# Scan of a hybrid decoder kernel on one Trainium2 core: step sizes loaded two chunks ahead, the sample sum ahead of the state decay on GpSimd, the first output tile's upper products first, the last convolution put off

## The chip, the cores and the metric

The kernel runs on one core of one Trainium2 chip. A core has five engines that each work through an instruction queue of their own, in order: TensorE (PE in the profile; its weight loads are PEld), VectorE (DVE), ScalarE (ACT), GpSimd (POOL) and SyncE (SP). They wait for one another by semaphores. SP and POOL issue the transfers between the chip's memory (HBM) and on-chip memory (SBUF), which 16 DMA engines carry out. Products come out in PSUM. The metric is the device time of one execution in microseconds (us); the median of the runs is compared.

## The reference: what is computed

One inference step of a small decoder trunk: a Mamba-2 (SSD) layer and a pooling layer, for 1024 new tokens of one sequence (the prompt) and 8 new tokens of each of 8 sequences (the samples), together 1088 token columns. The width is 1024, the inner width 2048, in 32 heads of 64 in 8 groups of 4, with a state of 128. All data are float32. The part of the reference that this case is about, cut:

```python
zxbcdt = h @ w_in                                # z, x, B, C, dt
conv = conv_b + sum(xp[:, k:k + L] * conv_w[k] for k in range(4)); xbc = silu(conv)
# scan, chunks of T = 128 tokens, for each group g of 4 heads
acum = cumsum(dt * A)                            # within a chunk
y_intra = einsum('bctgn,bcsgn->bctsg', C, B) * decay  @ xdt
chunk_states = einsum(B, exp(acum[-1] - acum), xdt)
h_c+1 = exp(acum[-1]) * h_c + chunk_states       # from chunk to chunk
y = y_intra + einsum(C, exp(acum), h_prev) + d_skip * x
gated = rmsnorm over the 256 columns of a group of (y * silu(z))
x = x + (1 + gate) * (gated @ w_out)
```

The samples' 64 columns are the ninth chunk (chunk 8): they start from given states h0 (8 sequences), which are decayed, added to and given back as new states.

## The kernel before, in words

Products in float32 are made of three products of rounded halves: upper times upper, lower times upper, upper times lower (`mm3`, lines 182 to 184; matmul weights wh and wl are the halves of a weight tile, gh and gl or hh and hl those of the activations). A product of 128 output rows has three column pieces of 368, 368 and 352 (CH), each in a PSUM tile `mm`, of which there are three.

The SSD layer runs group after group, 0 to 7 (`scan_group`). Beside the scan of groups 0 to 4, PE makes the input projection of later groups, each of four tiles (x, x, B, C) with a convolution on DVE and ACT behind it (`conv_tile`, lines 356 to 362; `proj_evict` moves the product out of PSUM on ACT, L419 and L421, and then calls `proj_end`, which makes the convolution). Beside the scan of groups 5 to 7, PE makes the output projection of the groups that are done, in parts of four k tiles (`op_units`, `op_unit`): for an output tile d and a column piece 12 matmuls, then the eviction into x on DVE (L771 to L776). The k tiles come back from HBM (gr), are split into gh on ACT (L749) and gl on DVE (L750), and the x tiles of the residual are loaded two output tiles ahead (L1528).

A group's scan takes its nine chunks two by two. For a chunk, `front` reads the step sizes (acb, a broadcast load of 256 KB, L533 and L536), makes exp of them on ACT (ea, L548), transposes on PE (tr, L554 and L557), masks the decay (M), scales x (xd) on DVE, and copies Bt out on ACT (L574); `states` sums the chunk states S (L596) and carries them on (hd on GpSimd, L604, then h on DVE, L605); `rows` makes the output rows y (L617, L621). For chunk 8 the columns are first copied into xp tiles on GpSimd (L436). `sample_inter` multiplies the given states with C (Z, L636) and scales (zsc on DVE, L639). `back_sample` adds xdt to zsc on GpSimd (L645), from which PE makes the samples' rows (L650), and decays the given states h0 on GpSimd, 128 x 1024 twice (L653). `state_sample` adds the samples' contributions to them (L670 on PE, L673 on DVE) and stores them (hsT, L675). The group's norm follows: y times z (L709), squares (L710), their sum (L711), its row sums ms on PE (L715), the rows' scale rs, which goes through HBM and comes back (L720, L723), and the scaled rows (L727).

Tiles of SBUF come from pools: a tile's buffer is given to the next tile of its tag when all readers of the old one are through, and a load into it waits for that. Large tiles (x, xbc, z, h0, gr, gh, gl) share slots, so that which tile comes after which depends on the order in which they are asked for and freed.

The order of instructions on each engine is set by a scheduler of the framework, which takes the instructions as the generators of scan and products issue them, turn by turn, weighs them with estimates of its own, and fixes one order for each engine; at run time an engine only waits. `issue_after(ins)` lays what is issued under it behind the instruction `ins`.

## Time and profile before

| | us |
|---|---|
| median of 3 runs | 1618.24 (1616.37 to 1619.92) |
| the profiled execution | 1620.23 |
| its span, first to last instruction | 1618.5 |
| PE busy | 1581.7 (98%) |
| DVE busy | 1288.2 (80%) |
| ACT busy | 796.5 (49%) |
| POOL busy | 500.8 (31%) |

The scan runs from about 330 to 950 us of the span. In the profile's timelines a row has the start in us, the duration, the engine, the line of the kernel, the operation, the tile written and those read, the sizes and the count; in brackets the idle time of the engine just before, and what ended it. Waits are rows of an engine and line, what was waited for, the sum in us, how often, and the longest. The granted clock is 1.00 at full speed.

### The profile page before, as it was taken

The numbers are of one execution on the slowest core, as the hardware profiler recorded it, in microseconds if no ns is written. First come the engines' busy times: TensorE is split into PE (matmuls) and PEld (weight loads), VectorE is DVE, ScalarE is ACT, GpSimd is POOL, SyncE is SP. The second block draws the span as 40 slices with busy tenths as digits, with TensorE's granted clock in tenths as the row PEclk, the third lists the DMA queues.
The fourth block names the chain that finished last, engine by engine and source line by source line (L and its number), as shares of the span: only waits on it lengthen the run. The fifth ranks groups of instructions, "written<-read, shape, count | busy, mean of one in ns | idle before, by whom it ended". The sixth has DMA issues, their size and how long they took to land. (4 is left out here: it accounts for less than half of the span.)

```text
span 1618.5 us, 30648 instructions
## 1 busy us (share of the span) xinstructions
PE 1581.7 (98%) x11916; PEld 1506.4 (93%) x11916; DVE 1288.2 (80%) x2148; ACT 796.5 (49%) x1517; POOL 500.8 (31%) x562
## 2 busy tenths in 40 slices
PE   8999999999999999999999999999999999999997
PEld 6799999998889889888898899999999999999997
DVE  5875779778888888788888867988889867577886
ACT  6653344357676766674555436623223233333364
POOL 0133556421221212120212222365666640000241
PEclk8999999999999999999999999999999999999999
DMA  9422232354555454668898632133333379555683
GB/s 344 169 85 91 94 117 69 110 186 139 201 161 175 157 192 148 234 210 300 293 338 279 216 128 93 45 139 115 106 106 103 115 223 364 164 165 180 160 176 120
DMA packets 122305, 275.58 MB, mean 170 GB/s; under 512 B 18192, under 2 KB 59312, under 8 KB 122160
## 3 DMA queue, kind: packets, MB, share of 16 engines
q1 hardware_dynamic: 118128, 260.90, 46.6%
q0 software_dynamic: 4032, 12.72, 4.5%
q8 instruction: 94, 1.54, 0.4%
q14 instruction: 51, 0.42, 0.1%
HBM read 201.12 MB, written 70.23 MB: 168 GB/s over the span
## 5 line engine op out<-in xcount | busy, mean ns | idle before, releaser
L989 PE MATMUL st<-hh,w 128*128 128x272 f32 x832 | 240.7, 289 | 2.1 <-DVE w L176 2.1
L987 PE MATMUL st<-hh,w 128*128 128x272 f32 x832 | 240.1, 289 | 0.0
L988 PE MATMUL st<-hl,w 128*128 128x272 f32 x832 | 239.9, 288 | 0.0
L987 PE MATMUL st<-t,w 128*128 128x272 f32 x624 | 179.7, 288 | 0.0
L989 PE MATMUL st<-t,w 128*128 128x272 f32 x624 | 179.5, 288 | 0.0
L182 PE MATMUL mm<-hh,wh 128*128 128x368 f32 (+1 forms) x528 | 178.7, 338 | 0.7 <-ACT raw L421 0.7
L988 PE MATMUL st<-t,w 128*128 128x272 f32 x624 | 179.2, 287 | 0.0
L183 PE MATMUL mm<-hl,wh 128*128 128x368 f32 (+1 forms) x528 | 173.6, 329 | 0.0
L184 PE MATMUL mm<-hh,wl 128*128 128x368 f32 (+1 forms) x528 | 173.4, 328 | 0.0
L989 PEld LDWEIGHTS st<-hh,w 128*128 128x128 f32 x832 | 156.4, 188 | 3.2 <-DVE w L176 3.2
L174 ACT ACTIVATE w<-wr 128x512 fp32r<-128x512 f32 x104 | 65.7, 631 | 188.8 <-PE st L989 155.5
L988 PEld LDWEIGHTS st<-hl,w 128*128 128x128 f32 x832 | 156.7, 188 | 0.0
L987 PEld LDWEIGHTS st<-hh,w 128*128 128x128 f32 x832 | 156.7, 188 | 0.0
L183 PE MATMUL mm<-gl,wh 128*128 128x368 f32 (+1 forms) x384 | 127.3, 331 | 3.6 <-DVE gl L750 3.5
L182 PE MATMUL mm<-gh,wh 128*128 128x368 f32 (+1 forms) x384 | 130.1, 340 | 0.6 <-ACT raw L419 0.5
L1204 PE MATMUL op<-b,w 128*128 128x272 f32 x448 | 128.9, 288 | 0.7 <-DVE b L1133 0.7
L1203 PE MATMUL op<-b,w 128*128 128x272 f32 x448 | 129.5, 289 | 0.0
L1205 PE MATMUL op<-b,w 128*128 128x272 f32 x448 | 128.9, 288 | 0.0
L184 PE MATMUL mm<-gh,wl 128*128 128x368 f32 (+1 forms) x384 | 127.0, 331 | 0.0
L604 POOL TENSOR_TENSOR hd<-h,cd 128x256 f32<-128x256 f32 x56 | 46.8, 836 | 233.2 <-DVE h L605 118.3
L987 PEld LDWEIGHTS st<-t,w 128*128 128x128 f32 x624 | 117.7, 189 | 0.1
L989 PEld LDWEIGHTS st<-t,w 128*128 128x128 f32 x624 | 117.3, 188 | 0.0
(298 smaller groups left out, 4544.6 us busy)
## 6 DMA issues: line engine op xcount, KB each, us to landing
wr<-win SPq DMA_DIRECT2D x48, 512.0 KB, 4.3
acb<-acd SPq DMA_DIRECT2D x64, 256.0 KB, 4.0
wr<-pin SPq DMA_DIRECT2D x32, 512.0 KB, 3.6
wr<-pout SPq DMA_DIRECT2D x28, 512.0 KB, 3.7
x<-x1d SPq DMA_DIRECT2D x24, 544.0 KB, 6.1
x1d<-x SPq DMA_DIRECT2D x22, 544.0 KB, 3.9
wr<-pout POOLq DMA_DIRECT2D x20, 512.0 KB, 5.7
x<-xT SPq DMA_DIRECT2D x16, 544.0 KB, 6.9
```

The costliest lines, as they stand in the source:

```text
L174: self.nc.scalar.activation(hi, src, AF.Copy)
L182: nc.tensor.matmul(ps[:, :n], hi[:, k, :], ah[:, a:a + n], start=first, stop=False)
L183: nc.tensor.matmul(ps[:, :n], hi[:, k, :], al[:, a:a + n], start=False, stop=False)
L184: nc.tensor.matmul(ps[:, :n], lo[:, k, :], ah[:, a:a + n], start=False, stop=last)
L604: nc.gpsimd.tensor_tensor(out=hd, in0=h[-1], in1=cd.unsqueeze(2).to_broadcast([P, 4, 64]), op=ALU.mult)
L987: nc.tensor.matmul(ps[c][:, :QUART], hi[:, k], xh[:, t], start=(k == 0), stop=False)
L988: nc.tensor.matmul(ps[c][:, :QUART], hi[:, k], xl[:, t], start=False, stop=False)
L989: nc.tensor.matmul(ps[c][:, :QUART], lo[:, k], xh[:, t], start=False, stop=(k == 3))
L1203: nc.tensor.matmul(ps[:, :QUART], hi[:, k], xh, start=k == 0, stop=False)
L1204: nc.tensor.matmul(ps[:, :QUART], hi[:, k], xl, start=False, stop=False)
L1205: nc.tensor.matmul(ps[:, :QUART], lo[:, k], xh, start=False, stop=k == 7)
```

## The change

It has five parts. (1) The step sizes acb get three buffers instead of two; two chunks are loaded at a group's start, and chunk c + 2 when chunk c is worked on. (2) The exponential ea is left out for chunk 0, where nothing reads it, and is made for chunk 8 on the 32 columns that are read; the three copies for chunk 8 go into the rest of that ea tile, so that they need the ring of ea and no tiles of their own. (3) In `back_sample` the add to zsc is issued first, and the two decays of h0 are laid behind it. (4) The first output tile (part 0, d = 0) is made by a new function, `op_first`: its three pieces at once, for each k tile the two products with the upper half of the activations, and only then the products with the lower halves. (5) The convolution of the last projected tile (group 6, the fourth) is not made behind its projection, but after output unit 7 of part 0 (the second piece of d = 2).

```diff
--- before.py
+++ after.py
@@ -24,6 +24,7 @@
 WINDOWS = tuple(2 << g for g in GROUPS)
 PARTS = ((0, 4), (4, 8), (8, 12), (12, 16))
 PREP = ((6, 10, 14, 18, 21), (9, 12, 15, 18, 21))
+LATE = 7
 XA = 2
 PLAIN = 2
 POOLW = (3, 5)
@@ -401,8 +402,9 @@
                     if k < 7:
                         yield
                 for c in range(3):
-                    self.proj_evict(G, ii, raw, ps[c], c)
+                    self.proj_evict(G, ii, raw, ps[c], c, False)
                 yield
+                self.late = lambda: self.proj_end(G, ii, raw, True)
                 return
             ada = self.ada_do(self.ada_plan[G["g"], ii]) if (G["g"], ii) in self.ada_plan else iter(())
             for c in range(3):
@@ -413,14 +415,15 @@
                     next(ada, None)
                 yield
 
-    def proj_evict(self, G, ii, raw, ps, c):
+    def proj_evict(self, G, ii, raw, ps, c, end=True):
         nc, (a, n) = self.nc, CH[c]
         pn = min(a + n, NP) - a
         nc.scalar.activation(raw[:, 3 + a:3 + a + pn], ps[:, :pn], AF.Identity)
         if pn < n:
             nc.scalar.activation(raw[:, 1027:1115].rearrange("p (b w) -> p b w", w=11)[:, :, 3:11],
                                  ps[:, pn:n].rearrange("p (b i) -> p b i", i=8), AF.Identity)
-            self.proj_end(G, ii, raw, True)
+            if end:
+                self.proj_end(G, ii, raw, True)
 
     def gate_chunk(self, dst, c, ps):
 
@@ -529,10 +532,10 @@
         def load_ac(c):
             if c < 8:
                 j, cc = c // 2, c % 2
-                t = gp.tile([P, 4, 128], F32, tag="acb", bufs=2, name=self.name("acb"))
+                t = gp.tile([P, 4, 128], F32, tag="acb", bufs=3, name=self.name("acb"))
                 nc.sync.dma_start(t, self.acd[32 * j + 4 * g:32 * j + 4 * g + 4, 128 * cc:128 * cc + 128].unsqueeze(0).to_broadcast([P, 4, 128]))
             else:
-                t = gp.tile([P, 4, 128], F32, tag="acb", bufs=2, name=self.name("acb"))[:, :, :64]
+                t = gp.tile([P, 4, 128], F32, tag="acb", bufs=3, name=self.name("acb"))[:, :, :64]
                 nc.sync.dma_start(t, self.acd[96 + 4 * g:100 + 4 * g, 256:320].unsqueeze(0).to_broadcast([P, 4, 64]))
             acbs[c] = t
 
@@ -543,11 +546,14 @@
             t0 = 128 * c
             tok = slice(t0, t0 + L)
             acb = acbs.pop(c)
-            load_ac(c + 1) if c < 8 else None
+            load_ac(c + 2) if c < 7 else None
             ea = gp.tile([P, 4, 128], F32, tag="ea", bufs=3, name=self.name("ea"))
-            nc.scalar.activation(ea[:, :, :L], acb, AF.Exp)
-            if c == 8:
-                xp = [gp.tile([P, 128], F32, tag=f"xp{i}", bufs=1, name=self.name("xp")) for i in range(3)]
+            if 0 < c < 8:
+                nc.scalar.activation(ea, acb, AF.Exp)
+            elif c:
+                xp = [ea[:, i + 1] for i in range(3)]
+                ea = ea[:, 0, :32].rearrange("p (r b) -> p r b", r=4)
+                nc.scalar.activation(ea, acb[:, :, 7:64:8], AF.Exp)
                 for i, t in enumerate((xs[0], xs[1], B)):
                     self.twice(xp[i], t[:, tok], nc.gpsimd)
             pt = pp.tile([P, 512], F32, tag="tr", bufs=2, name=self.name("tr"))
@@ -642,16 +648,18 @@
 
         def back_sample(F, xz):
             tok, M, xdt, xde, Bt, _, ea = F
-            nc.gpsimd.tensor_tensor(out=xz, in0=xz, in1=xdt, op=ALU.add)
+            ins = nc.gpsimd.tensor_tensor(out=xz, in0=xz, in1=xdt, op=ALU.add)
             for q in range(2):
                 py = pp.tile([P, 512], F32, tag="y", bufs=2, name=self.name("y"))
                 for rr in range(2):
                     r, o = 2 * q + rr, slice(64 * rr, 64 * rr + 64)
                     nc.tensor.matmul(py[o, :64], xz[:, r, :], M[:, r, :64], start=True, stop=True)
                 evac_y(py, q, tok, 64)
-            for i in range(2):
-                nc.gpsimd.tensor_tensor(out=h0[i], in0=h0[i],
-                                        in1=ea[:, :, 32 * i + 7:32 * i + 32:8].rearrange("p r b -> p b r").unsqueeze(3).to_broadcast([P, 4, 4, 64]), op=ALU.mult)
+            with self.tc.issue_after(ins.ins):
+                for i in range(2):
+                    nc.gpsimd.tensor_tensor(out=h0[i], in0=h0[i],
+                                            in1=ea[:, :, 4 * i:4 * i + 4].rearrange("p r b -> p b r").unsqueeze(3).to_broadcast([P, 4, 4, 64]),
+                                            op=ALU.mult)
 
             xv = xde.rearrange("p r q -> p (r q)")
             st = gp.tile([P, 256], F32R, tag="xl", bufs=1, name=self.name("st"))
@@ -676,6 +684,7 @@
                 self.slots.free(hsl[i])
 
         load_ac(0)
+        load_ac(1)
         F = [front(0)]
         yield
         F.append(front(1))
@@ -763,11 +772,30 @@
         out.append(self.op_split(st))
         yield
 
+    def op_first(self, l, x, d, w, acts):
+
+        nc, (hi, lo) = self.nc, w
+        ps = [self.mm_tile() for _ in CH]
+        for k, (ah, _) in enumerate(acts):
+            for c, (a, n) in enumerate(CH):
+                nc.tensor.matmul(ps[c][:, :n], hi[:, k, :], ah[:, a:a + n], start=(k == 0), stop=False)
+                nc.tensor.matmul(ps[c][:, :n], lo[:, k, :], ah[:, a:a + n], start=False, stop=False)
+            if k % 2:
+                yield
+        for c, (a, n) in enumerate(CH):
+            for k, (_, al) in enumerate(acts):
+                nc.tensor.matmul(ps[c][:, :n], hi[:, k, :], al[:, a:a + n], start=False, stop=(k == len(acts) - 1))
+            ins = self.op_evict(l, x, d, ps[c], CH[c])
+        yield ins
+
     def op_unit(self, l, x, d, w, acts, ch):
+        ps = self.mm_tile()
+        self.mm3(ps, w, acts, ch)
+        return self.op_evict(l, x, d, ps, ch)
+
+    def op_evict(self, l, x, d, ps, ch):
         nc, (a, n) = self.nc, ch
         pn = min(a + n, NP) - a
-        ps = self.mm_tile()
-        self.mm3(ps, w, acts, ch)
         ins = nc.vector.scalar_tensor_tensor(out=x[d][:, a:a + pn], in0=ps[:, :pn], scalar=self.gat[l][:, d, 8:9], in1=x[d][:, a:a + pn], op0=ALU.mult, op1=ALU.add)
         if pn < n:
             t = self.mt.tile([P, 64], F32, tag="gs", bufs=2, name=self.name("gs"))
@@ -1512,6 +1540,9 @@
             if p < 2:
                 self.prep = self.op_part_load(p + 1, self.acts[p + 1])
             for i, ins in enumerate(self.op_units(p)):
+                if p == 0 and i == LATE:
+                    with self.tc.issue_after(ins.ins):
+                        self.late()
                 if p < 2 and i in PREP[p]:
                     with self.tc.issue_after(ins.ins) if ins else contextlib.nullcontext():
                         next(self.prep, None)
@@ -1542,7 +1573,9 @@
             if d % 2 == 0:
                 ws = self.stream_pair()
             blk = self.ada_do(self.ada_late[p, d]) if (p, d) in self.ada_late else iter(())
-            for i, ch in enumerate(CH):
+            if p + d == 0:
+                yield from self.op_first(0, self.x, d, ws[0], self.acts[p])
+            for i, ch in enumerate(CH if p + d else ()):
                 ins = self.op_unit(0, self.x, d, ws[d % 2], self.acts[p], ch)
                 if i:
                     next(blk, None)
```

Three places of the order, in which the names are the tiles written and read; a row of PE's is a matmul, and the lines in the changed kernel are up to 30 higher than before.

On PE, at the first output tile, near 728 us of the span: ms is the norm's sum, mm the output pieces. Before:

```order
L715 MATMUL ms_8575<-z_8228,ones 32x272 [waits DVE_49]
L715 MATMUL ms_8575<-z_8228,ones 32x272 x3
L182 MATMUL mm_8586<-gh_8460,wh_8364 128x352
L183 MATMUL mm_8586<-gl_8461,wh_8364 128x352
L184 MATMUL mm_8586<-gh_8460,wl_8365 128x352
L182 MATMUL mm_8586<-gh_8473,wh_8364 128x352
L183 MATMUL mm_8523<-gl_8474,wh_8364 128x368 [waits DVE_49]
L184 MATMUL mm_8523<-gh_8473,wl_8365 128x368
L183 MATMUL mm_8561<-gl_8474,wh_8364 128x368
L184 MATMUL mm_8561<-gh_8473,wl_8365 128x368
```

and now:

```order
L781 MATMUL mm_8493<-gh_8453,wh_8344 128x352
L782 MATMUL mm_8493<-gh_8453,wl_8345 128x352
L724 MATMUL ms_8543<-z_8211,ones 32x272 [waits DVE_49]
L724 MATMUL ms_8543<-z_8211,ones 32x272 x3
L787 MATMUL mm_8491<-gl_8388,wh_8344 128x368
L787 MATMUL mm_8491<-gl_8403,wh_8344 128x368
L787 MATMUL mm_8491<-gl_8441,wh_8344 128x368
L787 MATMUL mm_8492<-gl_8388,wh_8344 128x368
L787 MATMUL mm_8491<-gl_8454,wh_8344 128x368 [waits DVE_49]
L787 MATMUL mm_8492<-gl_8403,wh_8344 128x368
```

The first wait for a lower half now comes behind all products of the upper halves; ms, which waits for DVE, stands behind 24 products of the first tile, and the last of the four lower halves is asked for behind it.

On POOL, at the end of group 5's scan: hd carries the state on, ctm are copies of C, h_163 and h_164 the given states. Before:

```order
L604 TENSOR_TENSOR hd_9164<-h_9159,cd_9118 128x256
L630 COPY ctm<-xbc_8041 128x4x8
L653 TENSOR_TENSOR h_163_9121<-h_163_9121,ea_9171 128x1024
L653 TENSOR_TENSOR h_164_9123<-h_164_9123,ea_9171 128x1024
L645 TENSOR_TENSOR zsc_9231<-zsc_9231,xd_9194 128x256
L631 COPY ctm<-xbc_8041 128x4x8
```

and now:

```order
L610 TENSOR_TENSOR hd_9139<-h_8984,cd_9010 128x256
L610 TENSOR_TENSOR hd_9143<-h_9138,cd_9097 128x256
L636 COPY ctm<-xbc_8026 128x4x8
L637 COPY ctm<-xbc_8026 128x4x8
L651 TENSOR_TENSOR zsc_9207<-zsc_9207,xd_9170 128x256
L660 TENSOR_TENSOR h_163_9100<-h_163_9100,ea_9150 128x1024
L660 TENSOR_TENSOR h_164_9102<-h_164_9102,ea_9150 128x1024
```

The add to zsc stands ahead of both decays, behind the two copies.

On DVE, in the scan of group 5 beside output tiles d = 2 and 3, near 748 us: raw is the convolution's sum, L799 an eviction, cb, M and xd the masks and scaled x of a chunk, L736 the norm's scaled rows. Before:

```order
L771 SCALAR_TENSOR_TENSOR x_8515<-mm_8735,gat_271,x_8515 128x368
L583 TENSOR_TENSOR ea_8767<-xbc_8337,ea_8767 128x512
L771 SCALAR_TENSOR_TENSOR x_8515<-mm_8751,gat_271,x_8515 128x368
L565 TENSOR_TENSOR cb_8780<-tr_8769,kc 128x128
L570 TENSOR_TENSOR xd_8783<-tr_8769,tkx_1435 128x512
L568 TENSOR_TENSOR M_8774<-M_8774,cb_8780 128x512
L771 SCALAR_TENSOR_TENSOR x_8515<-mm_8790,gat_271,x_8515 128x288
L774 TENSOR_TENSOR gs_8804<-mm_8790,gat_271 128x64
L727 SCALAR_TENSOR_TENSOR xbc_7441<-xbc_7441,vec,rs_8584 128x1088
L776 TENSOR_TENSOR x_8515<-x_8515,gs_8804 128x64
L727 SCALAR_TENSOR_TENSOR xbc_7600<-xbc_7600,vec,rs_8584 128x1088
L771 SCALAR_TENSOR_TENSOR x_8604<-mm_8814,gat_271,x_8604 128x368
```

and now:

```order
L799 SCALAR_TENSOR_TENSOR x_8483<-mm_8704,gat_271,x_8483 128x368
L736 SCALAR_TENSOR_TENSOR xbc_7425<-xbc_7425,vec,rs_8552 128x1088
L799 SCALAR_TENSOR_TENSOR x_8483<-mm_8720,gat_271,x_8483 128x368
L359 SCALAR_TENSOR_TENSOR raw_8737<-raw_8350,cwh,raw_8737 128x1112
L571 TENSOR_TENSOR cb_8761<-tr_8750,kc 128x128
L359 SCALAR_TENSOR_TENSOR raw_8737<-raw_8350,cwh,raw_8737 128x1112
L574 TENSOR_TENSOR M_8755<-M_8755,cb_8761 128x512
L359 SCALAR_TENSOR_TENSOR raw_8737<-raw_8350,cwh,raw_8737 128x1112
L576 TENSOR_TENSOR xd_8764<-tr_8750,tkx_1435 128x512
L799 SCALAR_TENSOR_TENSOR x_8483<-mm_8771,gat_271,x_8483 128x288
L802 TENSOR_TENSOR gs_8785<-mm_8771,gat_271 128x64
L736 SCALAR_TENSOR_TENSOR xbc_7584<-xbc_7584,vec,rs_8552 128x1088
```

The three sums of the convolution stand between the pieces of d = 2, ahead of M and xd of the chunk; the chunk's ea stands further back.

## The prediction

> **What bounds the kernel.** I read the page first, then the windows by stage, then TensorE's waits, then the timelines of the places where it waits.
>
> ```profile
> PE 1581.7 (98%) x11916; PEld 1506.4 (93%) x11916; DVE 1288.2 (80%) x2148; ACT 796.5 (49%) x1517; POOL 500.8 (31%) x562
> ```
>
> TensorE (PE) is the bound. The change removes no matmul, so only time in which PE idles or runs slowly can be won. The windows over the scan (start and end, length, busy us and instructions of PE, PEld, DVE, ACT, POOL, granted clock, DMA share, GB/s) tell where that is:
>
> ```profile
> 330.00:640.00 310.00, 309.46 (x2410) 280.20 (x2409) 254.37 (x401) 206.64 (x467) 68.48 (x128) 1.00 0.53 172
> 640.00:800.00 160.00, 152.99 (x1159) 138.10 (x1158) 137.19 (x225) 97.83 (x213) 31.50 (x50) 0.99 0.75 247
> 800.00:950.00 150.00, 145.01 (x1071) 135.06 (x1070) 125.48 (x239) 69.32 (x155) 25.36 (x28) 0.99 0.73 259
> ```
>
> Up to 640 PE idles 0.5 us: groups 0 to 3 have nothing to give. From 640 to 950 it idles 7.0 + 5.0 = 12.0 us. PE's waits from 300 to 1000 (total us, times, longest) name the causes:
>
> ```profile
> PE mm L183 <- DVE gl L750: 3.5, 2, 2.7
> PE y L650 <- POOL zsc L645: 2.9, 3, 1.9
> PE S L596 <- ACT Bt L574: 1.6, 1, 1.6
> PE Z L636 <- PE y L621: 1.5, 3, 0.9
> PE mm L182 <- ACT raw L421: 0.7, 1, 0.7
> PE y L617 <- DVE xd L570: 0.6, 1, 0.6
> PE tr L554 <- ACT Bt L574: 0.6, 1, 0.6
> ```
>
> Two stretches run at half the granted clock besides (0.50), each just after one of the two longest waits:
>
> ```profile
> 731.60:735.00 3.40, 2.84 (x11) 2.84 (x12) 3.40 (x4) 0.00 (x0) 0.00 (x0) 0.50 0.59 201
> 861.30:864.70 3.40, 3.40 (x14) 3.40 (x13) 2.01 (x4) 1.11 (x1) 0.00 (x0) 0.50 0.80 265
> ```
>
> Each costs half its length, 1.7 us. All these together are 14.8 us, the most that can be won.
>
> **Sample sum ahead of the decay.** At a group's end GpSimd runs both decays before the add that PE waits for:
>
> ```profile
> 854.76 0.41 DVE L639 TENSOR_TENSOR zsc<-Z,eap 128x256 f32<-128x256 f32 x1
> 853.96 4.17 POOL L653 TENSOR_TENSOR h<-h,ea 128x1024 f32<-128x1024 f32 x2 [0.26 <-PE Z L636]
> 858.09 1.76 POOL L645 TENSOR_TENSOR zsc<-zsc,xd 128x256 f32<-128x256 f32 x1
> 859.91 0.45 PE L650 MATMUL y<-M,zsc 128*64 128x64 f32 x8 [1.86 <-POOL zsc L645]
> 867.79 2.47 DVE L673 TENSOR_TENSOR h<-h,S 128x512 f32<-128x512 f32 x4
> ```
>
> The add's input is there at 854.76 + 0.41 = 855.17; put first, it ends by 855.17 + 1.76 = 856.9, and PE comes at 859.91 - 1.86 = 858.05. The wait goes, with 1.1 us to spare; beside other DVE work the add could take longer still and stay hidden. The decays then end at 856.9 + 4.17 = 861.1; who needs them is DVE's add at 867.79, 6.7 us later, so their delay costs nothing (were that cover gone, the state stores behind that add would be late next). The two small copies that now stand ahead of the add (0.2 us each) run while the add's input is still made. The clear cases are groups 5 to 7: 2.9 us, and with the 1.86 us idle the half-clock stretch behind it, 1.7: **4.6**. Ends: 2.9 (clock stays) and 4.6. I take 4.6, since the 1.58 us idle at 902.80 (below) is followed by no such stretch and this place will have none at all.
>
> The Trainium skill, "TensorE: Matmul & The Clock Gate", Part 1, says that a free-running window of about 3.4 us decides, and that the half rate comes after at least one idle window. The stretches are 3.4 us long, which agrees; the idle ahead of them was only 2.65 and 1.86 us, which does not: by the rule as written these idles would not have caused them, nothing would be won on the clock, and the sum below would be 3.4 lower.
>
> **Step sizes two chunks ahead.** The load of a chunk's step sizes (acb) is issued one chunk before its use:
>
> ```profile
> 889.98 0.37 SPq L533 DMA_DIRECT2D acb<-acd  x1
> 896.73 0.37 SPq L533 DMA_DIRECT2D acb<-acd  x1
> 902.37 0.21 ACT L582 ACTIVATE cd<-acb 128x4 f32<-128x4 f32 x1 [2.79 <-DMA acb<-acd]
> 902.80 0.70 PE L596 MATMUL S<-xd,Bt 128*128 128x256 f32 x2 [1.58 <-ACT Bt L574]
> 680.01 0.21 ACT L582 ACTIVATE cd<-acb 128x4 f32<-128x4 f32 x1 [1.19 <-DMA acb<-acd]
> 707.71 0.63 ACT L548 ACTIVATE ea<-acb 128x512 f32<-128x512 f32 x1 [1.75 <-DMA acb<-acd]
> 702.97 0.37 SPq L533 DMA_DIRECT2D acb<-acd  x1
> ```
>
> One chunk earlier means the place of the load before it: 6.75 us sooner, against ACT's wait of 2.79. So the 1.6 us goes, and the 0.6 of the transposes (ACT's wait 1.19) likewise. At 707.71 it does not: in the new order ACT asks there for the chunk after, whose load waits for the buffer of chunk 0 and so is issued near 703 again; ACT saves one skipped exponential (0.63) ahead of it, and I count 0.3 of PE's 0.7. Together **2.5** (ends 0, if SP holds the loads up, and 2.9). SP issues the same number of loads, but a group's start now has three: the third takes the buffer of the last chunk of the group before, waits for ACT's last read of it, and the weights and gr loads behind it on SP wait along. That is the end of 0. ACT's eight exponentials fewer are worth nothing: ACT is busy 49%.
>
> **First output tile: upper products first.**
>
> ```profile
> 721.88 0.43 PE L182 MATMUL mm<-gh,wh 128*128 128x368 f32 x1 [0.55 <-ACT raw L419]
> 725.51 0.44 PE L183 MATMUL mm<-gl,wh 128*128 128x368 f32 x1 [0.81 <-DVE gl L750]
> 726.53 1.28 DVE L711 TENSOR_TENSOR z<-z,z 128x1088 f32<-128x1088 f32 x1
> 730.82 1.29 DVE L750 TENSOR_TENSOR gl<-gr,gh 128x1088 fp32r<-128x1088 f32 x1 [3.01 <-issue]
> 732.16 0.68 PE L183 MATMUL mm<-gl,wh 128*128 128x368 f32 x1 [2.65 <-DVE gl L750]
> hsT<-h SPq DMA_DIRECT2D x2, 512.0 KB, 7.7
> 718.00:721.00 3.00, 3.00 (x20) 3.00 (x19) 2.02 (x4) 3.00 (x7) 0.00 (x0) 1.00 0.34 101
> 727.00:730.00 3.00, 2.51 (x19) 1.56 (x17) 0.81 (x1) 1.27 (x1) 0.00 (x0) 1.00 1.06 315
> ```
>
> The line on hsT is from the DMA issues of 715 to 732 (count, KB each, median us from issue to landing). The last lower half (gl) is written into the slot of a sample state whose store (hsT) must land first: 7.7 us in flight, it was issued near 723 and landed at 730.8, when DVE starts. Reordering matmuls moves no store: PE meets this wait with 8 lower products to do instead of 6. What helps is SP's order: one x load now stands ahead of both stores and falls into 718 to 721, where the DMAs are a third busy, and not into 727 to 730, where they are full. Half a megabyte at 315 GB/s is 1.7 us, and the next x load now waits behind the store instead of running beside it; I put the landing at or before 727.5. Then DVE is the last: L711 ends at 727.8, 0.5 earlier by ACT's earlier start, gl 1.28 later, 728.6. PE's walk: from 721.4 24 products of 0.166 and five transposes of 0.1, 725.9; it then waits 1.4 us for L711 (the norm's matmuls, ms, stand ahead of the lower products), does ms (0.5) and four lower products, and is at 728.5. Two things more are moved past queues here. The third mm tile now waits for an eviction that stands behind L710 on ACT, about 1 us, which is time that PE would else wait at ms. And the x load of the first tile goes into the slot of the other sample state, so that SP stands until that store has landed; it is wanted by the first eviction after 729. So 3.5 + 1.7 go and 1.4 comes: 3.8. An idle of 1.4 us lies below the 1.58 that left the clock whole. Ends: 0 (store lands as before) and 5.2. I take **3.8**, as the DMA rows are nearer to it.
>
> **The last convolution put off.** Its DVE work:
>
> ```profile
> 735.31 1.37 DVE L358 SCALAR_TENSOR_TENSOR raw<-raw,cwh,raw 128x1112 f32<-128x1112 f32 x1
> 739.37 1.22 DVE L360 SCALAR_TENSOR_TENSOR xbc<-raw,raw 128x1024 f32<-128x1024 f32 x1
> 749.00:757.00 8.00, 7.13 (x15) 1.00 0.94 306
> 757.00:765.00 8.00, 7.96 (x15) 1.00 0.81 271
> 752.50 1.34 DVE L727 SCALAR_TENSOR_TENSOR xbc<-xbc,vec,rs 128x1088 f32<-128x1088 f32 x1
> ```
>
> Three L358 and L360 are 5.3, with L362 5.5 us. They leave 732 to 741, where xd was late by 0.6 (won), and come near 750, DVE's busiest place: of 16 us it has 0.9 free. Up to 5.5 - 0.9 = 4.6 us of DVE work is late there. PE is covered in part: the new order puts the products of that chunk behind 13 matmuls more, and three mm tiles may wait for eviction. Ends: 0 and 4.6; I take 1.5, nearer to 0 for the moved products. Net **-0.9**. Its ACT share (L356, L359) lies in idle time. On SP the store of the first tile now stands ahead of the norm's load (rs); that tile is done some 5 us after 728.6, and rs is read at 752.50 (in the new order near 748), so 14 us are left for a load.
>
> **Chunk 8 copies.** They were a group ahead on GpSimd, in front of the last hd:
>
> ```profile
> 780.67 0.76 POOL L436 COPY xp<-xbc 128x128 f32<-128x128 f32 x3 [9.88 <-PE tr L557]
> 781.39 1.65 POOL L604 TENSOR_TENSOR hd<-h,cd 128x256 f32<-128x256 f32 x1
> ```
>
> Now they are this group's, in a ring of ea, ahead of the last or second last hd, with 9.88 us of free time before. hd may start up to 0.76 earlier: of Z's 1.5 I take **0.5** (ends 0 and 1.5).
>
> **Sum.** 4.6 + 2.5 + 3.8 - 0.9 + 0.5 = 10.5. The profiled execution took 1620.23 (span 1618.5 and 1.7 around it) and would take 1609.7; it lies 2.0 above the median of 1618.24, so the median becomes 1607.7.
>
> **Rivals.** (a) The store lands as before: the first tile brings 0, 1611.5. For it: the 7.7 us. Against: the emptier DMA before it. (b) The put-off convolution costs its whole 4.6: 1610.8. For it: 7.96 of 8. (c) The half clock comes by a beat of its own, not by idle: 3.4 less, 1611.1. For it: two equal lengths; against: both follow the longest idles, and the 1.58 drew none. That is what the Trainium skill's rule (above) comes to. (d) The loads come no earlier, as at 707.71: 1610.2. (e) Slower: the chunk 8 copies wait for their ring slot until the last reader is through, and hold up chunk 8's transposes and the last hd in each of eight groups. It decides from (10.5 + 3.2) / 8 = 1.7 us a group, which gives 1621.4. Against it stand the 9.88 us; for it, that groups 0 to 3, at 0.5 us of idle, have no slack seen.
>
> **How the numbers follow.** Chances: my forecast 0.40, (a) 0.16, (b) 0.13, (c) 0.09, (d) 0.07: all faster, 0.85. (a) and (b) together bring 10.5 - 3.8 - 3.1 = 3.6, 1614.6; that and worse within it, 0.05, is no change. (e) 0.10. A difference under 0.2% (3.2 us) counts as none, about what three runs between 1616.37 and 1619.92 can tell. Range: from all 14.8 won, 1603.4, to (a), (b) and (c's) second 1.7 together, 1616.3.
>
> **What would show it.** Right: PE's waits from 300 to 1000 without zsc, S and xd; clock 1.00 throughout 640 to 950; a wait of about 1.4 us at ms near 725 and none over 0.5 at gl; PE idle there about 4. Wrong: gl still behind "issue" near 730; new waits on M, xd, h or mm slots between 745 and 765; tr waiting for POOL.

## The result: 0.39% faster, and the profile after

The changed kernel takes 1611.5 us (median of 10 runs, 1609.0 to 1613.4) beside 1617.9 for the kernel before (10 runs on the same chip): ratio 0.9961, 95% interval 0.9952 to 0.9971, so 6.4 us less where 10.5 were forecast. Its profiled execution took 1612.66, span 1610.9. Two later repetitions on another chip gave 1611.43 and 1611.67, ratios 0.9945 and 0.9949: there the change wins 8.2 and 7.9, so 6.4 is the least of three readings.

TensorE's work is the same; what it loses between matmuls is less. The engine line of the page, then the three windows of the scan that the prediction showed for before:

```profile
PE 1581.8 (98%) x11916; PEld 1505.7 (93%) x11916; DVE 1291.5 (80%) x2148; ACT 790.6 (49%) x1509; POOL 507.4 (31%) x562
```

```profile
330.00:640.00 310.00, 309.51 (x2418) 280.76 (x2416) 255.16 (x405) 202.07 (x458) 74.24 (x127) 1.00 0.52 173
640.00:800.00 160.00, 155.92 (x1175) 139.12 (x1172) 139.81 (x227) 99.15 (x217) 31.47 (x48) 1.00 0.76 255
800.00:950.00 150.00, 148.51 (x1101) 138.28 (x1100) 127.63 (x243) 70.22 (x157) 28.74 (x33) 1.00 0.73 257
```

From 640 to 950 PE idles 4.1 + 1.5 = 5.6 us where it idled 12.0, and the clock is 1.00 throughout: both half-clock stretches are gone. That is 6.4 + 3.4. Yet the scan of this execution became only 7.8 shorter (next table), so some 2 us were lost where the profile shows no wait (1.6 and 2.7 in the two other executions). PE's waits from 300 to 1000 (total us, times, longest):

```profile
PE mm L183 <- ACT raw L423: 1.3, 1, 1.3
PE am L263 <- ACT mp L259: 1.3, 1, 1.3
PE mm L787 <- DVE gl L759: 0.9, 1, 0.9
PE pl L183 <- ACT hh L320: 0.7, 1, 0.7
PE S L602 <- ACT Bt L580: 0.6, 1, 0.6
PE mm L781 <- ACT raw L423: 0.5, 1, 0.5
PE y L623 <- DVE M L574: 0.5, 1, 0.5
```

The waits for zsc, xd and tr are gone, that for S has shrunk from 1.6 to 0.6, that for gl from 3.5 to 0.9. Of the two at the top, the one for mp is new. The one for raw stood in the list of before with 0.7 (there ScalarE had waited 1.75 for acb, the row at 707.71 of the prediction); it has doubled, and its cause has changed. Nothing in the prediction named that cause. ScalarE's, GpSimd's and TensorE's timelines at those two places show it:

```profile
704.70 1.06 POOL L651 TENSOR_TENSOR zsc<-zsc,xd 128x256 f32<-128x256 f32 x1 [0.41 <-DVE zsc L645]
705.72 4.29 POOL L660 TENSOR_TENSOR h<-h,ea 128x1024 f32<-128x1024 f32 x2
710.04 0.63 ACT L552 ACTIVATE ea<-acb 128x512 f32<-128x512 f32 x1 [2.42 <-POOL h L660]
710.87 0.22 ACT L423 ACTIVATE raw<-mm 128x64 f32<-128x64 f32 x1
711.14 0.43 PE L183 MATMUL mm<-hh,wh 128*128 128x352 f32 x1 [1.33 <-ACT raw L423]
790.79 0.63 ACT L552 ACTIVATE ea<-acb 128x512 f32<-128x512 f32 x1 [4.40 <-POOL h L660]
791.43 0.36 ACT L259 ACTIVATE mp<-am 128x256 f32<-128x256 f32 x1
791.85 0.61 PE L263 MATMUL am<-kc,mp 128*128 128x9 f32 x4 [1.30 <-ACT mp L259]
```

The add now goes first, so the two decays (L660) start later, by its length at least, 1.06 here and 1.59 near 784. They read chunk 8's factors, which lie in a buffer of the ring of three ea tiles. The next group's chunk 3 gets that buffer, and its exponential stands on ScalarE ahead of an eviction that PE waits for. ScalarE has the same wait of 2.42 at the ends of groups 0 to 3 (417 to 637), where it costs PE nothing: PE idles 0.5 from 330 to 640, as before.

Where the time went can be read closely by taking the same matmuls in two profiled executions: the first st matmul of the last tile before the scan (341.6 in before), the Z matmuls of groups 4, 5, 6 and 7 (702.1, 784.0, 853.2, 914.3) and an st matmul behind the scan (1066.0). Each number is by how much the stretch between two of them differs from before, in us. The changed kernel stands there three times (the third is the run skip0), which shows how far single executions of one program differ: 0.2 in the second and third stretch, 0.4 in the fourth, about 1 in the first and last. The kernel before stands for one execution alone, 2.0 above its median, and what is particular to that execution is in every row.

| Kernel | Whole scan | to 702 | 702–784 | 784–853 | 853–914 | 914–1066 |
|---|---|---|---|---|---|---|
| changed | −7.8 | −1.2 | −2.3 | +0.5 | −4.4 | −0.4 |
| changed, 2nd and 3rd execution | −5.4, −6.9 | −0.3, −0.8 | −2.4, −2.3 | +0.6, +0.5 | −4.0, −4.0 | +0.9, −0.4 |
| nozsc | −4.6 | −1.7 | −3.1 | +1.2 | −1.8 | +0.8 |
| zsc | −0.5 | +1.6 | −0.4 | −0.2 | −0.5 | −0.9 |
| own8 | −4.0 | +1.1 | −2.5 | −1.2 | −0.6 | −0.8 |
| nolate | −1.6 | −1.1 | +0.1 | +2.0 | −2.1 | −0.6 |
| nofirst | −1.2 | −1.5 | −3.2 | +4.9 | −0.7 | −0.7 |
| noac | −3.1 | −0.8 | −1.1 | −1.2 | +0.8 | −0.9 |
| c3i | −8.3 | −0.3 | −2.8 | −1.0 | −4.1 | −0.1 |
| c3e | −9.6 | −1.0 | −3.7 | −1.2 | −3.3 | −0.6 |
| late10 | −7.0 | −0.3 | −3.9 | +0.7 | −3.4 | −0.1 |
| both | −10.8 | −0.4 | −4.0 | −1.2 | −4.4 | −0.8 |

Three things limit what the table tells. The Z matmuls do not cut every kernel at the same work: beside the kernel before, four matmuls of the output projection (0.17 us each) stand ahead of the Z at 784 and not behind it in the changed kernel, nozsc, c3i and late10, two in nofirst, six in own8 and noac, eight in c3e and both. Between kernels of unequal counts up to 1.3 us pass from the third stretch to the second; the sum of the two holds. In the second execution, nolate, nofirst, c3i and c3e the last stretch holds 3.41 us at half clock at 1004 to 1012, behind the scan, which cost 1.7 (last section). And a row is one execution: that of nofirst is the slowest of its twelve (1621.3, median 1615.3), those of own8, zsc and nozsc lie 4.0, 2.8 and 2.4 below their medians.

The other kernels are the experiments below. Their times, each with the kernel before on the same chip:

| Kernel | Median us (runs) | Before beside it | Ratio, 95% interval |
|---|---|---|---|
| nozsc | 1616.6 (12) | 1618.9 | 0.9979, 0.9968 to 0.9990 |
| zsc | 1619.2 (12) | 1618.9 | 1.0000, 0.9989 to 1.0011 |
| own8 | 1618.0 (12) | 1618.9 | 0.9994, 0.9981 to 1.0007 |
| nolate | 1615.9 (12) | 1618.9 | 0.9986, 0.9976 to 0.9996 |
| changed, again | 1611.4 (6) | 1619.6 | 0.9945, 0.9930 to 0.9959 |
| skip0 | 1611.7 (5) | 1619.6 | 0.9949, 0.9937 to 0.9961 |
| nofirst | 1615.3 (12) | 1619.6 | 0.9970, 0.9956 to 0.9984 |
| noac | 1616.9 (10) | 1619.6 | 0.9984, 0.9972 to 0.9997 |
| c3i | 1610.0 (5) | 1618.3 | 0.9951, 0.9939 to 0.9963 |
| c3e | 1608.3 (6) | 1618.3 | 0.9945, 0.9931 to 0.9960 |
| late10 | 1609.9 (5) | 1618.3 | 0.9947, 0.9934 to 0.9960 |
| both | 1606.1 (5) | 1617.7 | 0.9922, 0.9908 to 0.9936 |

### The profile page after: what moved, and what is told of

Read it like the earlier page. It is cut to its first block, busy times and chain, and to the rows that moved or that the text cites. A ratio compares the mean times of both kernels' runs of the same rounds, so it can differ in the third digit from the quotient of the medians.

```text
span 1610.9 us, 30644 instructions
## 1 busy us (share of the span) xinstructions
PE 1581.8 (98%) x11916; PEld 1505.7 (93%) x11916; DVE 1291.5 (80%) x2148; ACT 790.6 (49%) x1509; POOL 507.4 (31%) x562
## 4 chain that ended last, share of the span: by engine, by line
PE 86%; DVE 5%; issue 3%; DMA 2%; ACT 1%; POOL 1%; SPq 0%; DVEq 0%; POOLq 0%; ACTq 0%
PE st L1017 11%; PE st L1015 11%; PE st L1016 11%; PE mm L183 11%; PE mm L184 10%; PE mm L185 10%; PE op L1232 2%; PE op L1233 2%; PE op L1231 2%; PE y L623 2%; PE S L602 2%; PE y L627 2%; PE am L254 1%; PE tr L563 1%; PE tr L560 1%
## 5 line engine op out<-in xcount | busy, mean ns | idle before, releaser
L183 PE MATMUL mm<-gh,wh 128*128 128x368 f32 (+1 forms) x372 | 125.6, 339 | 0.1
L184 PE MATMUL mm<-gl,wh 128*128 128x368 f32 (+1 forms) x372 | 122.2, 329 | 0.1
L185 PE MATMUL mm<-gh,wl 128*128 128x368 f32 (+1 forms) x372 | 122.2, 328 | 0.0
```

What stands on the lines that cost most here:

```text
L183: nc.tensor.matmul(ps[:, :n], hi[:, k, :], ah[:, a:a + n], start=first, stop=False)
L184: nc.tensor.matmul(ps[:, :n], hi[:, k, :], al[:, a:a + n], start=False, stop=False)
L185: nc.tensor.matmul(ps[:, :n], lo[:, k, :], ah[:, a:a + n], start=False, stop=last)
```

## Experiments

A line number in a profile of these kernels can lie up to three off the changed kernel's; those of zsc are the kernel before's, at most one off. One thing has to be kept in mind with all of them: the kernel's order of work is laid by a scheduler, and most edits make it lay some of the scan anew. Where an edit left TensorE's order as it was (nozsc, c3i), it tells one cause alone; elsewhere it tells the cause and a new order together.

### The add ahead of the decays, left out (nozsc)

```diff
-            with self.tc.issue_after(ins.ins):
-                for i in range(2):
-                    nc.gpsimd.tensor_tensor(out=h0[i], in0=h0[i],
+            for i in range(2):
+                nc.gpsimd.tensor_tensor(out=h0[i], in0=h0[i],
```

Only GpSimd's order differs from the changed kernel's; those of the four other engines are equal.

> The changed kernel with the decays issued as before, without the add laid ahead of them. Theory: TensorE's waits for zsc are back (2.9 us and the half clock behind the longest, 1.7: 4.6), but the decays end earlier, so that ScalarE's waits for the ea slot shrink and TensorE wins about 1.3 to 2.0 back: 2.6 to 3.3 us slower than the changed kernel. Rival: the slot wait has nothing to do with it; then 4.6 us slower.

Measured: 1616.6, ratio 0.9979 against 0.9945 to 0.9961 for the changed kernel. PE's waits, TensorE's rows at two of the group ends, and windows behind each of these two:

```profile
PE y L656 <- POOL zsc L651: 5.7, 3, 2.2
786.63 0.45 PE L656 MATMUL y<-M,zsc 128*64 128x64 f32 x8 [2.19 <-POOL zsc L651]
856.39 0.45 PE L656 MATMUL y<-M,zsc 128*64 128x64 f32 x8 [1.86 <-POOL zsc L651]
786.60:790.00 3.40, 3.37 (x28) 3.30 (x29) 3.28 (x6) 2.87 (x7) 0.37 (x1) 1.00 0.93 267
857.85:861.26 3.41, 3.41 (x13) 3.41 (x13) 2.06 (x4) 1.11 (x1) 0.00 (x0) 0.50 1.01 314
```

Without the add ahead the waits for zsc are 5.7 in sum and one half-clock stretch comes back, 7.4 us together; yet the scan is only 2.1 longer than the mean of the changed kernel's three executions (−4.6 against −6.7), and 3.5 from 702 on, beside the two executions without half clock behind the scan. From 702 to 784 it is even 0.8 shorter: the decays end earlier there and hold ScalarE less (its waits for them at the two places fall from 2.42 to 1.48 and from 4.40 to 1.98, PE's waits behind them from 1.3 to 0.4 and from 1.3 to none). From 784 to 853 it is 0.7 longer although a wait of 2.2 has come back there. So the add put ahead wins its waits and pays for part of them, 0.8 + 1.5 = 2.3, at the other end of the decays. The times alone can't tell the theory from the rival: by the ratios nozsc is 2.9 to 5.5 slower than the changed kernel, which takes in 2.6 to 3.3 and 4.6 alike.

ScalarE's waits for the decays do not vanish here, and the kernel before has none at these places: there the exponential waits for acb (1.75 at 707.71, 0.59 at 792.53). The step sizes' earlier loads uncover the wait for the buffer; the later decays lengthen it.

### The add ahead of the decays, alone (zsc)

The kernel before with this one part of the change:

```diff
-            nc.gpsimd.tensor_tensor(out=xz, in0=xz, in1=xdt, op=ALU.add)
+            ins = nc.gpsimd.tensor_tensor(out=xz, in0=xz, in1=xdt, op=ALU.add)
...
-            for i in range(2):
+            with self.tc.issue_after(ins.ins):
+                for i in range(2):
```

> The kernel before, with nothing changed but the add laid ahead of the decays. Theory: 4.6 us won (2.9 and 1.7 of clock), less what the later decays cost through ScalarE's wait for the ea slot near 710 and 790: 2.5 to 4 us faster than before. Rival, as the prediction had it: the later decays cost nothing, 4.6 us.

Measured: 1619.2, ratio 1.0000, no gain. PE's waits show why:

```profile
PE y L621 <- DVE h L601: 4.9, 5, 1.9
PE mm L183 <- DVE gl L751: 3.4, 2, 2.6
PE y L617 <- DVE xd L570: 1.7, 1, 1.7
```

No wait for zsc is left, and 4.9 us of waits for h, which the kernel before didn't have, stand in their place, with one half-clock stretch (883.6 to 887.0). By itself the part that the forecast priced at 4.6 brings nothing measurable, neither the theory's 2.5 to 4 nor the rival's 4.6: the order around it was laid anew, and other things became late. No exponential waits for the decays here (near 708 and 790 those of the next group wait for acb, 1.50 and 1.02), so this run says nothing for or against the ring.

### Chunk 8's factors in a tile of their own (own8)

```diff
-                ea = ea[:, 0, :32].rearrange("p (r b) -> p r b", r=4)
+                ea = gp.tile([P, 4, 8], F32, tag="e8", bufs=1, name=self.name("e8"))
```

> The changed kernel, with chunk 8's 32 decay factors in a small tile of their own instead of in the ring of ea. Theory: in the changed kernel the decays of h0, now behind the add, hold chunk 8's ea tile until they end, and the exponential of the next group's third chunk on ScalarE waits for that slot (2.42 us at 710, 4.40 us at 791); TensorE waits 1.3 us for ScalarE each time. With a tile of their own both waits go: ScalarE never waits for POOL L660, and 2.2 to 2.6 us are won on the changed kernel (about 1609). Rival: the exponential would wait at the same place for its step sizes' load, as it did before; then the wait changes its name, and under 0.7 us is won.

Measured: 1618.0, ratio 0.9994. As the theory has it, no exponential waits for L660 any more, the am wait near 791 is gone, and the stretch 784 to 853 is 1.7 shorter than in the changed kernel (0.3 of it is two matmuls that have passed to the stretch before). Near 707 the rival is right in part: the exponential waits 1.28 for its step sizes where it waited 2.42 for L660, and PE's wait for raw falls from 1.3 to 0.5. But by the ratios the time is 5.3 to 7.9 above the changed kernel's. In the new order chunk 8's exponential stands ahead of Bt on ScalarE, and there it waits for its step sizes:

```profile
895.97 0.26 ACT L556 ACTIVATE e<-acb 128x32 f32<-128x32 f32 x1 [3.26 <-DMA acb<-acd]
PE S L602 <- ACT Bt L580: 2.9, 3, 2.2
```

Behind the 2.2 us wait for Bt half clock follows (897.1 to 900.5), and 853 to 914 loses 3.6. The mechanism holds at the place near 791, but this is no way to use it.

### A buffer fewer in the ring (skip0)

```diff
-            ea = gp.tile([P, 4, 128], F32, tag="ea", bufs=3, name=self.name("ea"))
+            ea = gp.tile([P, 4, 128], F32, tag="ea", bufs=3, name=self.name("ea")) if c else None
```

> The changed kernel, but chunk 0, which never uses its ea buffer, takes none: the ring of three then comes round one chunk later, and the first exponential that needs the buffer of the group before's chunk 8 is chunk 3's, not chunk 2's. All five engines get the same instructions in the same order. Theory (an exponential on ScalarE waits for GpSimd's later decays, and TensorE for the evictions behind it): ScalarE's waits for GpSimd L660 at 710.0 (2.42) and 790.8 (4.40) go, TensorE's waits of 1.3 for raw and mp go with them, and the time is 2.0 to 3.0 below the changed kernel's. Rival 1 (the next late thing takes their place, such as gl behind its store near 730 and the mp copy behind another instruction): 0 to 1.0 below. Rival 2 (the waits were for something else that the profile puts down to GpSimd): the two waits stand, no difference.

Measured: 1611.7 beside 1611.4, and ScalarE's wait stands:

```profile
708.91 0.63 ACT L552 ACTIVATE ea<-acb 128x512 f32<-128x512 f32 x1 [2.42 <-POOL h L660]
```

The idea was wrong: by the unchanged order, chunk 0's buffer, into which nothing is written, never held a place in the ring. The edit changes neither an order nor a wait, and the waiting exponential was chunk 3's already (the third of its group in the timeline). So this run is a repetition and stands as one in the table; the ring theory is neither helped nor hurt.

### Chunk 3's exponential issued later (c3i, c3e)

The other way to keep ScalarE from standing there: leave the ring alone and issue the waiting instruction behind others. In c3i for group 6 (the place near 791), in c3e for groups 5 and 6, as shown:

```diff
-            if 0 < c < 8:
+            if 0 < c < 8 and not (c == 3 and g in (5, 6)):
                 nc.scalar.activation(ea, acb, AF.Exp)
-            elif c:
+            elif c == 8:
...
-            nc.scalar.activation(M[:, :, :L], M[:, :, :L], AF.Exp, scale=-1.0)
+            ins = nc.scalar.activation(M[:, :, :L], M[:, :, :L], AF.Exp, scale=-1.0)
+            if c == 3 and g in (5, 6):
+                with self.tc.issue_after(ins.ins):
+                    nc.scalar.activation(ea, acb, AF.Exp)
```

> The changed kernel, but in group 6 the exponential of chunk 3 is issued behind that chunk's mask exponential, so that ScalarE no longer stands before it while GpSimd decays the states. TensorE's and GpSimd's orders are those of the changed kernel; a few rows of ScalarE, VectorE and SyncE behind 787 change places. Theory (slot wait of chunk 3): ScalarE's wait of 4.40 for GpSimd L660 near 790.8 goes, TensorE's delay of 1.47 at am near 791.9 falls below 0.3, and the time is 1.0 to 1.5 below the changed kernel's. Rival (what ScalarE does then is late in its turn: the later ea, the masks or the x load that SyncE now issues earlier): the am delay goes and another of 1 or more comes between 792 and 830; within 0.5 of the changed kernel.

> The same in groups 5 and 6. In group 5 the schedule after 707 is laid anew in part (some 150 rows of TensorE's order, 350 of VectorE's). Theory: TensorE's delays at 711.1 (1.49) and 791.9 (1.47) both go, and the time is 2.0 to 3.0 below the changed kernel's. Rival 1 (at 711 the gain is given back at gl, which waits for its store and not for ScalarE): 1.0 to 1.5 below. Rival 2 (the new order costs what the wait cost): within 1 of the changed kernel, with new waits between 711 and 790.

Measured: 1610.0 and 1608.3. c3i has TensorE's order of the changed kernel, and the am wait is missing from its list. ScalarE's timeline there:

```profile
786.29 0.38 ACT L259 ACTIVATE mp<-am 128x256 f32<-128x256 f32 x1 [1.39 <-PE am L254]
```

mp now waits for PE, not PE for mp, and 784 to 853 is 1.0 shorter than before, not 0.5 longer: 1.5 won, the size that the theory gave, with TensorE's order unchanged. In c3e both waits go (0.2 is left of the one for raw); the top of its list:

```profile
PE S L605 <- ACT Bt L583: 1.5, 1, 1.5
PE y L626 <- DVE M L577: 0.8, 1, 0.8
```

702 to 784 wins 1.4 and 784 to 853 1.7 on the changed kernel: 3.1 together, which with the four matmuls that have passed from the later stretch to the earlier is some 2.1 and 1.0. That is three quarters of the gap between the forecast of 10.5 and the 6.4 measured first. In group 5 the order is new, so only the 1.5 of c3i is the wait alone. The ratios alone (0.9951, 0.9945) don't part these kernels from the changed one on other chips (0.9945 to 0.9961); the traces do.

### The old order in the first output tile (nofirst)

```diff
-            if p + d == 0:
-                yield from self.op_first(0, self.x, d, ws[0], self.acts[p])
-            for i, ch in enumerate(CH if p + d else ()):
+            for i, ch in enumerate(CH):
```

> The changed kernel with the first output tile in the old order of products; the put-off convolution, the loads and the add ahead of the decays stay. Theory of the forecast (the tile's own order and what it moves on SyncE's queue bring 3.8): the wait for gl is back near 730 at 2 us or more with a half-clock stretch behind it, 3 to 5 above the changed kernel. Rival (the gain near 720 to 740 came from the put-off convolution alone, which frees VectorE ahead of gl and xd): gl waits under 1.2, no half clock, 0 to 1.5 above. As the order near 745 to 760 changes too, up to 1 either way is not told apart.

Measured: 1615.3, 3.8 above the changed kernel beside it. The total is what the forecast's theory says, the place is not:

```profile
PE S L602 <- ACT Bt L580: 3.8, 3, 1.8
PE am L263 <- ACT mp L259: 2.3, 1, 2.3
PE mm L183 <- ACT raw L423: 1.3, 1, 1.3
PE mm L184 <- DVE gl L759: 1.1, 1, 1.1
789.70:796.50 6.80, 6.65 (x26) 5.59 (x27) 5.07 (x9) 4.69 (x10) 0.00 (x0) 0.51 0.74 264
```

In the first tile gl waits 1.1 without half clock, as the rival has it, and 702 to 784 is 0.9 shorter than with the new order (0.3 of it is two matmuls fewer). The loss lies behind it: the am wait near 790 grows from 1.3 to 2.3, and half clock follows for 6.8 us, twice the length of any other such stretch here (3.4 us lost), so that 784 to 853 is 4.4 longer; then the wait for Bt, 3.8. So the tile's order wins nothing in the tile. Why undoing it makes am and Bt later could not be told apart from the order that was laid anew behind 784. Nor is it known how much of the 6.8 us at half clock the other eleven executions have: this one took 6.1 us more than their median.

### The convolution back at its place (nolate)

```diff
-                    self.proj_evict(G, ii, raw, ps[c], c, False)
+                    self.proj_evict(G, ii, raw, ps[c], c)
...
-                self.late = lambda: self.proj_end(G, ii, raw, True)
...
-                if p == 0 and i == LATE:
-                    with self.tc.issue_after(ins.ins):
-                        self.late()
```

> The changed kernel with the last convolution at its old place. Theory: the put-off convolution brings no wait of TensorE, but the finer order beside it costs about 2 us in changes between kinds of matmul (733 to 783: the starts lie 9.8 us apart beyond the matmuls' own time, against 7.6 before without its two waits), and it saves the 0.8 us wait for xd: undoing it wins 0 to 1.2 us. Rival: it made room for the first output tile, and undoing it loses 1.5 us or more, at xd and gl.

Measured: 1615.9, ratio 0.9986. TensorE's waits, VectorE's timeline and the window behind it:

```profile
PE y L622 <- DVE xd L575: 2.9, 1, 2.9
726.97 1.36 DVE L359 SCALAR_TENSOR_TENSOR raw<-raw,cwh,raw 128x1112 f32<-128x1112 f32 x1
...
730.34 1.36 DVE L359 SCALAR_TENSOR_TENSOR raw<-raw,cwh,raw 128x1112 f32<-128x1112 f32 x1
731.63 0.68 DVE L575 TENSOR_TENSOR xd<-tr,tkx 128x512 f32<-128x512 f32 x1
733.49:736.90 3.41, 3.41 (x13) 3.41 (x12) 2.40 (x7) 3.41 (x8) 0.00 (x0) 0.50 1.03 348
```

With the convolution at its old place its three sums stand on VectorE between gl and xd, PE waits 2.9 us for xd, and half clock follows. gl was done just before them, and PE's largest wait for it is 0.2. So the gain near 730 belongs to the convolution: put off, it makes 702 to 784 and 784 to 853 shorter by 2.4 and 1.5 (3.9 together). The theory, that undoing it wins, is out; the rival holds for xd, while gl shows no loss.

### The convolution put off further (late10)

```diff
-LATE = 7
+LATE = 10
```

> The changed kernel with the put-off convolution laid behind output unit 10 instead of 7, some 10 us later. Theory (what the put-off convolution costs is the VectorE work itself, 5.5 us of it wherever it stands between 740 and 790, and TensorE's finer changes of kind): within 0.8 of the changed kernel. Rival 1 (its place near 745 to 752, VectorE's busiest, costs about 1.5): 1 to 2 below. Rival 2 (later is too late: its products or VectorE's rows of the next chunks come late): 1 or more above, with a wait for M, xd or h between 755 and 790.

Measured: 1609.9, ratio 0.9947, which doesn't part it from the changed kernel. 702 to 784 is 1.6 shorter, with the same number of matmuls; the scan as a whole is not clearly shorter (−7.0, where the changed kernel has −5.4 to −7.8). In the windows of the changed kernel's second execution, and then of late10, PE is busy throughout in both:

```profile
740.00:752.00 12.00, 12.00 (x89) 11.26 (x88) 11.86 (x17) 8.50 (x19) 0.00 (x0) 1.00 0.87 313
752.00:764.00 12.00, 12.00 (x89) 9.54 (x88) 11.30 (x23) 4.59 (x14) 1.54 (x2) 1.00 0.78 254
```

```profile
740.00:752.00 12.00, 12.00 (x96) 11.56 (x95) 11.45 (x21) 6.07 (x18) 1.54 (x2) 1.00 0.86 312
752.00:764.00 12.00, 12.00 (x97) 10.28 (x95) 11.79 (x18) 8.43 (x18) 0.00 (x0) 1.00 0.85 319
```

No wait is listed there in either. The loss sits in starts a tenth or two of a microsecond late. Between the first tile and the next Z (some 50 us), by the start times in the traces, the starts of the matmuls are later than their predecessors' sizes ask for by 10.2 us in the changed kernel, 9.0 in late10, and 8.2 in before without its two listed waits there; at changes of kind (from y to mm and the like) it is 3.3 in 32, 2.6 in 23 and 2.0 in 20. So the put-off convolution does cost about 2 us in the changed kernel, as small starts and not as a wait, and its place decides over most of it: rival 1 by this stretch, though not by the time of the kernel. That the changes of kind are the cause was not tried by itself; they account for some 60% of the differences.

### The loads one chunk ahead again (noac)

```diff
-                t = gp.tile([P, 4, 128], F32, tag="acb", bufs=3, name=self.name("acb"))
+                t = gp.tile([P, 4, 128], F32, tag="acb", bufs=2, name=self.name("acb"))
...
-            load_ac(c + 2) if c < 7 else None
+            load_ac(c + 1) if c < 8 else None
...
-        load_ac(1)
```

> The changed kernel with two step-size buffers and each load one chunk ahead, as before the change; the rest stays. Theory of the forecast (the loads bring 2.5): waits for Bt or ea that ScalarE has from the DMA of acb are back, 1.0 or more at one place and 2 to 3 in sum, and the time is 2 to 3 above the changed kernel's. Rival 1 (the loads were hidden in the new order too): no wait of ScalarE for acb above 1 shows at TensorE, within 1 of the changed kernel. Rival 2 (the edit lays the whole scan's order anew, and that weighs more than the loads): a difference of either sign beyond 3, with waits that have nothing to do with acb.

Measured: 1616.9, 5.4 above the changed kernel beside it, 3.6 by the scan. ScalarE's rows and PE's wait:

```profile
875.81 0.63 ACT L552 ACTIVATE ea<-acb 128x512 f32<-128x512 f32 x1 [2.96 <-DMA acb<-acd]
898.58 0.21 ACT L588 ACTIVATE cd<-acb 128x4 f32<-128x4 f32 x1 [2.91 <-DMA acb<-acd]
PE S L602 <- ACT Bt L580: 3.4, 2, 1.9
```

ScalarE waits 3 us for acb twice, Bt stands behind it, PE loses 3.4 and a half-clock stretch besides (899.2 to 902.6): 853 to 914 is 4.9 longer. The loads did what the forecast said, at the named place. How much of the 3.6 is theirs and how much the new order's stays open: no exponential waits for L660 in this order, and PE waits 1.6 for an eviction at 732, which the changed kernel doesn't.

### The two edits, c3e and late10, together (both)

c3e with LATE = 10.

> The two edits that each won alone, together: chunk 3's exponential behind its mask in groups 5 and 6 (1608.3 alone), and the put-off convolution behind output unit 10 (1609.9 alone, 1.5 below the changed kernel). Theory (they win at different places, 711 and 792 the one, 745 to 783 the other): the second win of 1.5 adds to the first, 1606.8. Rival (behind the earlier evictions at 711 the convolution was no longer late, so its place is worth nothing more): 1608.3, within 0.7.

Measured: 1606.1, ratio 0.9922, interval 0.9908 to 0.9936. Its windows:

```profile
640.00:800.00 160.00, 158.57 (x1198) 142.13 (x1200) 140.96 (x233) 99.39 (x216) 34.98 (x48) 1.00 0.77 260
800.00:950.00 150.00, 148.93 (x1102) 139.01 (x1102) 126.41 (x241) 72.02 (x160) 30.96 (x35) 1.00 0.74 259
```

PE idles 2.5 us from 640 to 950. The time is below the theory's 1606.8, yet the trace speaks for the rival: 702 to 784 is −4.0, only 0.3 below c3e, so at its own place the later convolution hardly added to the first edit. The rest came from 853 to 914, where the wait for Bt is 0.3 here and 1.5 in c3e. That wait differs between executions of one kernel too (0.6 and 1.1 in two of the changed kernel), so it can't be put down to the edit.

## Why the forecast came out as it did

Faster was forecast and measured, and 1611.5 lies in the range; the size was not met: 10.5 was forecast, 6.4 measured (8.2 and 7.9 in the repetitions, 5.4 to 7.8 by the scan in single executions). That the time lies in the range is in part luck: the first term was too high, the last two too low, and the errors offset each other in part. Nor can a part's worth be added up from its undoing: nozsc, noac, nofirst and nolate lose 2.1, 3.6, 5.5 and 5.1 of the scan, 16.3 in sum, where all the parts together win 6.7. One sum counts a little twice: of the first half-clock stretch 0.56 us is idle that already stands in the 3.5 of gl, so it costs 1.4 and not 1.7. By terms:

- **Sample sum ahead of the decay, 4.6.** The three waits went, the half clock at 861 too. The step that failed is "their delay costs nothing". VectorE's add at 867.79 was taken for the only one who needs the decays' end; but they also hold the buffer of ea that they read, and the next group's chunk 3 waits for it with evictions behind. The delay costs 2.3 by nozsc, 0.8 and 1.5 at two places; taking the exponential out of the way there wins 1.5 at the one alone (c3i) and 3.1 at both (c3e). What is left of the term is 2.1 to 3.5 by nozsc's trace. At the first place the prediction looked (its row at 707.71) and expected a load's wait there; what came was GpSimd's 2.42.
- **Step sizes, 2.5.** Right in place and cause; noac shows 3.6 for it in the scan, the new order included. The one thing missed is that S still waits 0.6 to 1.1.
- **First output tile, 3.8.** The sum at the place came out near, the cause did not. The forecast let the store land by 727.5 because the DMAs were a third busy from 718 to 721. In the new order they are full there: the last load of gr is issued at 715.88 where it was at 714.58, and those of acb and x at 717.43 and 718.57 where they were at 718.85 and 719.34. So gl starts at 729.48, 1.3 earlier than before and not 3.5:

```profile
718.00:721.00 3.00, 3.00 (x20) 3.00 (x19) 2.94 (x5) 2.55 (x4) 0.00 (x0) 1.00 0.95 303
729.48 1.29 DVE L759 TENSOR_TENSOR gl<-gr,gh 128x1088 fp32r<-128x1088 f32 x1 [1.29 <-issue]
726.26 0.43 PE L781 MATMUL mm<-gh,wh 128*128 128x352 f32 x1 [0.55 <-ACT raw L423]
```

  The gl wait is 0.9, the wait of 1.4 at ms is 0.4 (0.9 and 0.4 in the two other executions), and the third mm tile waits 0.5 for its eviction, where about 1 was said. nofirst shows that the tile's order wins nothing here (0.6 to 0.9 is lost), though undoing it costs 4.4 further on, in the one execution traced, by a way that stays open.
- **The put-off convolution, −0.9.** The sign was wrong. The 1.5 of lateness near 750 is there in size (about 2, of which late10 wins 1.6 back), but as small starts, not as waits for M or xd. What it brings was priced at the 0.6 of xd in the old trace; nolate shows 3.9 for 702 to 853. In the old order gl was so late that xd hardly mattered: with the gl wait gone, xd would have been next, 2.9 us and half clock. The step did not ask what is late next after the wait that the other term removed.
- **Chunk 8, 0.5.** The waits for Z fell from 1.5 to 0.3: 1.2. No run tried this part by itself.

Of the rivals, (c) is out as it was put: with the idle gone the half clock is gone from the scan (though a beat has a part in it, last section). (a) names 1611.5 to the tenth, but by luck: the first tile's wait did not stay, and gl came 1.3 earlier. (b) is out: the put-off convolution costs about 2 and not 4.6. (d) is out, as the wait for S shrank. (e) saw the ring and asked only who waits to enter it; who waits for it to be left is what cost. The signs named beforehand held for zsc, xd and the clock. S still waits, the 0.9 at gl exceeds the 0.5 allowed, the 1.4 at ms is 0.4, and PE idles 5.6 from 640 to 950 where about 4 was said.

## What to carry to other kernels

When work on an engine is moved later, list everyone who waits for its end: the readers of what it writes, and the next owner of every buffer that it reads. When several waits lie close together, price each removal with the others gone, since the next wait behind it may be the larger one and belong to another part of the change. And where a scheduler lays the order, a part that wins in the whole can win nothing alone (zsc), so a part's worth is read by undoing it where the other engines' orders stay.

## What was not expected of the hardware

**Half clock.** Idle of about 2 us was followed by half clock at some places and not at others: in nozsc 1.86 at 856 was, 2.19 at 786 wasn't, nor 2.60 at 732 in zsc. Every such stretch lasts 3.4 us, but the one in nofirst 6.8. The longest idle ahead of any of them is 2.9 (nolate), so the Trainium skill's rule of "TensorE: Matmul & The Clock Gate", Part 1 (half rate after at least one idle window of about 3.4 us), differs from what is measured.

Where the idle falls has a part in it. In each trace all changes of the granted clock lie whole steps of 3.41 us apart. Behind the scan every kernel has the same wait of 1.92 us at the same matmul. In the changed kernel's second execution it falls into one step, and half clock follows; in its first a boundary divides it, and none follows:

```profile
1003.02:1006.43 3.41, 1.45 (x8) 0.89 (x7) 1.76 (x6) 2.32 (x8) 2.66 (x9) 1.00 0.00 0
1006.43:1009.84 3.41, 3.41 (x13) 3.41 (x13) 3.41 (x14) 3.41 (x13) 1.27 (x3) 0.50 0.02 5
1002.70:1006.11 3.41, 2.51 (x16) 2.21 (x14) 2.74 (x7) 0.90 (x4) 3.28 (x10) 1.00 0.00 0
1006.11:1009.52 3.41, 2.37 (x13) 2.00 (x14) 2.42 (x9) 3.41 (x11) 1.46 (x5) 1.00 0.00 0
```

Cut into such steps, the 14 traces hold, from 35 us on and without each trace's last 10 us, 16 steps in which PE idles 1.76 us or more by the profile. Half clock follows 15 of them; one of 1.87 (nozsc, 1004.62) has none behind it. Of the steps with less idle (up to 1.72), half clock follows two, both in nofirst, among them the second half of its 6.8 us. So in these traces half clock came with about half a step of idle, and not a whole one; no run moved an idle to try it.

**Late starts without a wait.** With PE busy 12.00 of 12.00 us the same work can still take 1.2 us longer in 50 (the changed kernel against late10). A list of waits doesn't show that; starts of the same instruction in two traces do.
